# Mixture of experts on one core: the transposes of the activations queued behind the preceding down product, and the 64-slot blocks from the third block on

## The chip, the cores and the metric

The kernel is one program on one core of a Trainium2 chip. The core has a matrix engine (TensorE, PE in the rows; PEld are its weight loads), a vector engine (VectorE, DVE), a scalar engine (ScalarE, ACT), GpSimd (POOL), and SyncE (SP), which here issues nearly all weight transfers. Each engine works through its own instructions in order; between engines they wait for one another by semaphores. The metric is the device time of one launch in microseconds (us), lower is better.

## What is computed

The reference is a chain of three transformer blocks over 256 tokens of width 1024. The change touches the last stage alone, a mixture of 8 experts with 2 experts per token:

```
logits = h @ router
top_v, top_i = lax.top_k(logits, 2)
gates = sum(one_hot(top_i) * softmax(top_v))
for e in range(8):
    out = out + gates[..., e:e+1] * ((silu(h @ we_gate[e]) * (h @ we_up[e])) @ we_down[e])
```

Each expert has three weight matrices of 1024 x 3584 (we_gate, we_up) and 3584 x 1024 (we_down) in float32.

## The kernel before

**Precision.** A large product is done in three matmuls of a fast float type: a weight tile `raw` is split into a rounded high part `whi` (ScalarE, line 306) and the remainder `wlo` (VectorE, line 307), and the activations likewise into two parts. `split_w` does this for a transferred tile of 1 MB in two pieces of 128x1024. The pool of `whi` and `wlo` has 4 buffers each, so a fifth split waits until the matmuls that read the first are done.

**Experts.** The routing decides which tokens go to which expert; each expert takes 128 slots (kind F) or 64 slots (kind N), sorted so that the experts with more tokens get the F places. Of 8 experts 4 are F and 4 are N. Each expert is cut into 7 blocks of 512 hidden columns, so there are 28 F blocks and 28 N blocks. An F block uses the three-matmul form with split weights. An N block uses the float32 weights as they are transferred, in one slower matmul each, and has no splits.

**One block** (function `experts`, one turn of the loop) is: the gate product into `g` (`up_proj`, 2 transfers of 1 MB), the up product into `up` (2 transfers), then the down product **of the block before** into `y` (`down_proj`, 2 transfers), then silu of `g` (ScalarE, line 290, tile `act`) and its product with `up` (VectorE, line 1615, `act`). The activations must be turned for the down product: `act_split` transposes `act` on TensorE into `aT` (line 1642; 4 transposes for F, 2 for N), and copies the result to `an` (N, ScalarE line 1645) or splits it into `ah` (ScalarE line 1649) and `al` (VectorE line 1650) (F). In the kernel before, `act_split` of a block is called in the next turn, between that block's gate and up product, and `ah` is tied behind the first split of that time (`splits_done[LEAD]`).

**Order of blocks.** `seq` starts with HEAD F blocks, then alternates N and F, and ends with the N blocks that are left. Before the first N block the kernel must have sorted the experts (`order`, a chain of some 30 small VectorE instructions on tile `so`), gathered the tokens of the second expert (`one_hots`, tile `sel`; `gather`, 32 matmuls into `xe`), and read the sorted expert numbers into registers of SyncE (`values_load`, line 1623), since all but the first expert's weights are addressed by them. The transfers that follow this read in SyncE's order can't be issued before it.

**What sets the order.** A scheduler orders each engine's instructions from the program's order, priorities and readiness; `issue_after` adds an edge that keeps the instructions of a `with` block behind a given one on its own engine. It costs no instruction. Transferred tiles live in a ring of 12 buffers of 1 MB (15 until the turn `i == HEAD`).

A second pass of the same code for experts with too many tokens is behind a branch and is not run.

Of the kernel before, what the change touches and what calls it, by code (L numbers as in the profile page):

```python
# [11 lines left out]
F32 = mybir.dt.float32  # L12
# [3 lines left out]
AF = mybir.ActivationFunctionType  # L16
OP = mybir.AluOpType
# [9 lines left out]
KINDS = "FNFNFNFN"  # L27
GROUPS = ((0,), (1,), (2, 3), (4, 5), (6, 7))
TAGS = ("u", "u", "x2", "u", "x2")
HEAD = 3  # L30
PE_TAPS = 13
EARLY = 7
PRE = 2
# [3 lines left out]
MORE = 2  # L37
EARLY_RAW = 5
FIRST = 3
LEAD = 0  # L40
HT0 = 1
PB = {"A": 3, "S": 2, "T": 1, "P": 2}
UB = {"u": 22, "u2": 10, "h": 8, "x2": 8}
# [166 lines left out]
class Build:  # L210
# [86 lines left out]
    def split_w(self, raw, n):  # L297

        nc = self.nc
        out = []  # L300
        self.splits_done = []
        for o in range(0, n, 1024):
            w = min(1024, n - o)
            hi = self.wpool.tile([128, 1024], R32, name="whi", tag="whi")
            lo = self.wpool.tile([128, 1024], R32, name="wlo", tag="wlo")
            self.splits_done.append(nc.scalar.activation(hi[:, :w], raw[:, o:o + w], AF.Copy))  # L306
            nc.vector.tensor_tensor(lo[:, :w], raw[:, o:o + w], hi[:, :w].bitcast(F32), op=OP.subtract)  # L307
            out.append((hi, lo))
        return out

# [1239 lines left out]
    def down_proj(self, e, b, act, yp):  # L1550
        nc = self.nc
        for part in range(2):
            raw = self.load_w(self.weights("we_down", e, 2 * b + part))
            if KINDS[e] == "N":
                for k in range(2):
                    st = act[:, k * 128 + part * 64:k * 128 + part * 64 + 64]
                    for n in range(2):
                        nc.tensor.matmul(yp[0][64 * n:64 * n + 64, :], st,  # L1558
                                         raw[:, k * 1024 + n * 512:k * 1024 + (n + 1) * 512],
                                         start=b == 0 and part == 0 and k == 0, stop=b == 6 and part == 1 and k == 1)  # L1560
                continue
            ah, al = act
            w = self.split_w(raw, 2048)
            for k in range(2):
                kk = part * 2 + k
                sh, sl = ah[:, kk * 128:(kk + 1) * 128], al[:, kk * 128:(kk + 1) * 128]
                for n in range(2):
                    h, l = (t[:, n * 512:(n + 1) * 512] for t in w[k])
                    for q, (s, m) in enumerate(((sh, h), (sl, h), (sh, l))):
                        nc.tensor.matmul(yp[n], s, m, start=b == 0 and kk == 0 and q == 0,  # L1570
                                         stop=b == 6 and kk == 3 and q == 2)

    def experts(self, rnd, nxt):


        nc = self.nc
        blocks = {k: [(e, b) for e in range(8) if KINDS[e] == k for b in range(7)] for k in "FN"}
        seq = blocks["F"][:HEAD]
        for n, f in zip(blocks["N"], blocks["F"][HEAD:]):
            seq += [n, f]  # L1580
        seq += blocks["N"][28 - HEAD:]
        at = {group[0]: g for g, group in enumerate(GROUPS)}
        early = {seq.index((group[0], 0)) - (2 if g == 1 else AHEAD): g for g, group in enumerate(GROUPS) if g}
        back, state, xes, yps, done = {}, {0: nxt}, {}, {}, None
        last = None
        for i, (e, b) in enumerate(seq):
            kind = KINDS[e]
            if b == 0:
                yps[e] = [self.ps("y0", "S")] + ([self.ps("y1", "P")] if kind == "F" else [])
                if e in at:  # L1590
                    sel, xe = state[at[e]]
                    for m in GROUPS[at[e]]:
                        xes[m] = xe
            pg = self.pa("g")
            self.up_proj("we_gate", e, b, xes[e], pg)
            if b == 0 and i and e in at:
                back.update(self.back(at[e], sel, TAGS[at[e]]))
            if last:
                act = self.act_split(*last[:2])
            pu = self.pa("up")  # L1600
            self.up_proj("we_up", e, b, xes[e], pu)
            if i == 0:
                back.update(self.back(0, sel, TAGS[0]))
            if done:
                self.combine(*done)
                done = None
            if last:
                self.down_proj(last[0], last[2], act, yps[last[0]])
                if last[2] == 6:
                    done = last[0], yps[last[0]], back[last[0]]  # L1610
            gs = back[e][1]
            w = 512 if kind == "F" else 256
            t = self.stile("act")[:, 0:w]
            self.gate_act(t, pg[:, 0:w], AF.Silu, scale=gs[1])
            nc.vector.scalar_tensor_tensor(t, pu[:, 0:w], gs[1], t, op0=OP.mult, op1=OP.mult)  # L1615
            last = (e, t, b)
            if rnd == 0 and i == 0:
                self.order()
            if i in early:
                g = early[i]  # L1620
                state[g] = self.gather(g, self.one_hots(g, rnd, TAGS[g]), TAGS[g])
            if rnd == 0 and i == HEAD - 2:
                self.ids = [None] + [nc.values_load(self.ci[0:1, p:p + 1], engines=[mybir.EngineType.SP],
                                                    min_val=0, max_val=7) for p in range(1, 8)]
            if rnd == 0 and i == HEAD:
                self.over = nc.values_load(self.ci[0:1, 8:9], min_val=0, max_val=256)
                self.first.__exit__(None, None, None)
                self.ring = [p for p in self.ring if p is not self.rpool3]
                self.epool = self.late.enter_context(self.tc.tile_pool(name="e", bufs=1, reuse_waits="tile"))
        act = self.act_split(*last[:2])  # L1630
        if done:
            self.combine(*done)
        self.down_proj(last[0], last[2], act, yps[last[0]])
        self.combine(last[0], yps[last[0]], back[last[0]])

    def act_split(self, e, t):

        nc = self.nc
        pt = self.ps("aT", "T")
        m = 4 if KINDS[e] == "F" else 2  # L1640
        for k in range(m):
            nc.tensor.transpose(pt[:, k * 128:(k + 1) * 128], t[:, k * 128:(k + 1) * 128], self.con("ident"))  # L1642
        if m == 2:
            an = self.stile("an")
            nc.scalar.activation(an[:, 0:256], pt[:, 0:256], AF.Copy)
            return an
        ah, al = self.stile("ah", dt=R32), self.stile("al", dt=R32)
        with self.tc.issue_after(self.splits_done[LEAD].ins):
            nc.scalar.activation(ah, pt, AF.Copy)  # L1649
        nc.vector.tensor_tensor(al, pt, ah.bitcast(F32), op=OP.subtract)  # L1650
        return ah, al

# [44 lines left out]
```

## Time and profile before

| | us |
|---|---|
| median of 3 runs (lowest, highest) | 1925.13 (1917.29, 1928.01) |
| profiled execution, its own time | 1928.41 |
| its span, first to last instruction | 1926.6 |

The mixture of experts takes the span from about 1011 us to the end. The profile gives the busy time and waits of each engine; a wait is named "engine tile line <- engine tile line", who waited and what ended the wait. "x" counts instructions. PEclk is the granted clock of TensorE as a share of full speed.

### The profile page before, as it was taken

The page shows a single profiled execution, that of the slowest core. Times are in us where ns is not written, and L with a number is a line of the kernel's source. Part 1 is how long each engine was busy: PE and PEld are TensorE (multiplying, and loading weights), DVE is VectorE, ACT ScalarE, POOL GpSimd, SP SyncE. Part 2 cuts the span into 40 slices and gives each one's busy share as a digit, 9 for nine tenths or more (in the row PEclk, how much of TensorE's full clock was granted, in tenths as well). Part 3 has the DMA queues.
Part 4 walks back from the last instruction along what each step waited for, and adds up shares of the span by engine and source line. Part 5 has one row for each costly group of instructions (what it writes and reads, how often), then busy time and mean ns, then how long its engine had stood idle before and what let it go on. Part 6 is the DMA issues. An engine that isn't in the chain of part 4 may idle for free. (4 is left out here: it accounts for less than half of the span.)

```text
span 1926.6 us, 30904 instructions
## 1 busy us (share of the span) xinstructions
PE 1849.0 (96%) x12304; PEld 1517.2 (79%) x12304; DVE 1209.3 (63%) x1814; ACT 963.9 (50%) x1429; POOL 10.9 (1%) x30
## 2 busy tenths in 40 slices
PE   7999999999999999999999999999999999999997
PEld 7989998889999889999788666666665657665654
DVE  7689797765568966655669545655464646454532
ACT  5545555554455774445657444444444435353531
POOL 0000000000000000000000000000000000000000
PEclk9999999999999999999999999999999999999999
DMA  8765566345553235557263999999999999999994
GB/s 300 267 245 198 205 255 245 135 153 178 196 177 119 104 121 186 184 174 256 87 241 130 420 420 421 390 402 393 399 378 388 382 384 390 368 412 371 403 394 162
DMA packets 77657, 531.31 MB, mean 276 GB/s; under 512 B 9283, under 2 KB 10051, under 8 KB 15425
## 3 DMA queue, kind: packets, MB, share of 16 engines
q1 hardware_dynamic: 75168, 524.66, 70.6%
q0 software_dynamic: 1328, 3.29, 0.9%
q8 instruction: 98, 1.61, 0.3%
q10 hardware_dynamic: 1008, 1.31, 0.2%
q14 instruction: 55, 0.44, 0.1%
HBM read 526.60 MB, written 2.62 MB: 275 GB/s over the span
## 5 line engine op out<-in xcount | busy, mean ns | idle before, releaser
L307 DVE TENSOR_TENSOR wlo<-raw,whi 128x1024 fp32r<-128x1024 f32 x618 | 725.1, 1205 | 279.7 <-ACT whi L306 277.1
L306 ACT ACTIVATE whi<-raw 128x1024 fp32r<-128x1024 f32 x618 | 626.8, 1044 | 367.2 <-PE lin L326 249.6
L326 PE MATMUL lin<-hh,whi 128*128 128x256 f32 x1248 | 356.2, 286 | 10.3 <-ACT whi L306 8.1
L326 PE MATMUL lin<-hh,wlo 128*128 128x256 f32 x1248 | 353.5, 284 | 1.8 <-DVE wlo L307 1.8
L326 PE MATMUL lin<-hl,whi 128*128 128x256 f32 x1248 | 353.7, 284 | 0.3
L326 PEld LDWEIGHTS lin<-hh,whi 128*128 128x128 f32 x1248 | 236.8, 190 | 15.4 <-ACT whi L306 9.1
L326 PEld LDWEIGHTS lin<-hh,wlo 128*128 128x128 f32 x1248 | 237.0, 190 | 4.0 <-DVE wlo L307 2.5
L326 PEld LDWEIGHTS lin<-hl,whi 128*128 128x128 f32 x1248 | 237.5, 190 | 2.8 <-issue 1.5
L1547 PE MATMUL g<-whi,xe 128*128 128x512 f32 x448 | 139.4, 392 | 0.3 <-DVE so L1392 0.3
L1547 PE MATMUL up<-whi,xe 128*128 128x512 f32 x448 | 139.5, 392 | 0.0
L1615 DVE SCALAR_TENSOR_TENSOR act<-up,gs,act 128x512 f32<-128x512 f32 (+1 forms) x56 | 34.6, 617 | 165.8 <-PE up L1539 128.1
L1570 PE MATMUL y<-whi,ah 128*128 128x512 f32 x224 | 94.3, 421 | 29.8 <-ACT whi L306 29.8
L1558 PE MATMUL y<-raw,an 128*64 128x512 f32 x448 | 106.7, 603 | 0.0
L1539 PE MATMUL up<-raw,xn 128*64 128x256 f32 x896 | 103.1, 380 | 0.0
L1539 PE MATMUL g<-raw,xn 128*64 128x256 f32 x896 | 102.8, 382 | 0.0
L1649 ACT ACTIVATE ah<-aT 128x512 fp32r<-128x512 f32 x28 | 16.7, 595 | 166.3 <-PE aT L1642 166.3
L1547 PEld LDWEIGHTS g<-whi,xe 128*128 128x128 f32 x448 | 83.9, 188 | 18.8 <-ACT whi L306 0.4
L1547 PEld LDWEIGHTS up<-whi,xe 128*128 128x128 f32 x448 | 84.0, 188 | 17.7
L290 ACT ACTIVATE act<-g,gs 128x512 f32<-128x512 f32 (+1 forms) x56 | 32.5, 581 | 122.2 <-PE g L1539 81.9
L1570 PE MATMUL y<-whi,al 128*128 128x512 f32 x224 | 91.4, 408 | 0.0
L1539 PEld LDWEIGHTS up<-raw,xn 128*64 128x64 f32 x896 | 63.5, 137 | 33.0 <-issue 0.9
L1547 PE MATMUL up<-wlo,xe 128*128 128x512 f32 x224 | 89.2, 398 | 0.0
(467 smaller groups left out, 3193.6 us busy)
## 6 DMA issues: line engine op xcount, KB each, us to landing
raw<-we_gate SPq DMA_DIRECT2D x112, 1024.0 KB, 7.9
raw<-we_up SPq DMA_DIRECT2D x112, 1024.0 KB, 8.6
raw<-we_down SPq DMA_DIRECT2D x112, 1024.0 KB, 7.3
raw<-w_in SPq DMA_DIRECT2D x35, 1024.0 KB, 6.2
raw<-w_ff SPq DMA_DIRECT2D x32, 1024.0 KB, 4.9
raw<-ada_w SPq DMA_DIRECT2D x24, 1024.0 KB, 4.9
raw<-cv_w_gate SPq DMA_DIRECT2D x11, 1024.0 KB, 4.8
raw<-cv_w_up SPq DMA_DIRECT2D x11, 1024.0 KB, 4.8
```

The source lines that it names most:

```text
L290: self.last_gate = self.nc.scalar.activation(*args, **kw)
L306: self.splits_done.append(nc.scalar.activation(hi[:, :w], raw[:, o:o + w], AF.Copy))
L307: nc.vector.tensor_tensor(lo[:, :w], raw[:, o:o + w], hi[:, :w].bitcast(F32), op=OP.subtract)
L326: nc.tensor.matmul(o, s, m, start=start and n == 0, stop=stop and n == 2, skip_group_check=True)
L1539: nc.tensor.matmul(ps[64 * h:64 * h + 64, 0:256], xe["N"][:, kk, :], raw[:, k * 512 + h * 256:k * 512 + (h + 1) * 256], start=kk == 0, sto ...
L1547: nc.tensor.matmul(ps, s, m, start=n == 0, stop=n == 23)
L1558: nc.tensor.matmul(yp[0][64 * n:64 * n + 64, :], st, raw[:, k * 1024 + n * 512:k * 1024 + (n + 1) * 512], start=b == 0 and part == 0 and k ...
L1570: nc.tensor.matmul(yp[n], s, m, start=b == 0 and kk == 0 and q == 0, stop=b == 6 and kk == 3 and q == 2)
L1615: nc.vector.scalar_tensor_tensor(t, pu[:, 0:w], gs[1], t, op0=OP.mult, op1=OP.mult)
L1649: nc.scalar.activation(ah, pt, AF.Copy)
```

## The change

The call of `act_split` moves from the next turn to the end of the block's own turn, right behind the product that makes `act`. So that the transposes are not put ahead of the down product that is emitted just before, they and the N copy `an` get edges behind that product's last matmul and, where it was an F block's, behind the last `whi` of its splits (`self.queued`). The N blocks' `act` on VectorE gets an edge behind the last `wlo` of these splits (`self.low_done`). The tie of `ah` to a split goes. HEAD becomes 2, so that the sequence is F F, then 26 times N F, then N N (before: F F F, 25 times N F, N N N).

```
-HEAD = 3
+HEAD = 2
...
-LEAD = 0
...
-            nc.vector.tensor_tensor(lo[:, :w], raw[:, o:o + w], hi[:, :w].bitcast(F32), op=OP.subtract)
+            self.low_done = nc.vector.tensor_tensor(lo[:, :w], raw[:, o:o + w], hi[:, :w].bitcast(F32), op=OP.subtract)
...
-                        nc.tensor.matmul(yp[n], s, m, start=b == 0 and kk == 0 and q == 0,
-                                         stop=b == 6 and kk == 3 and q == 2)
+                        self.downs = nc.tensor.matmul(yp[n], s, m, start=b == 0 and kk == 0 and q == 0,
+                                                      stop=b == 6 and kk == 3 and q == 2)
...
-        last = None
+        last, self.queued = None, []
...
-            if last:
-                act = self.act_split(*last[:2])
             pu = self.pa("up")
...
                 self.down_proj(last[0], last[2], act, yps[last[0]])
+                self.queued = [self.downs] + ([self.splits_done[-1]] if KINDS[last[0]] == "F" else [])
...
             self.gate_act(t, pg[:, 0:w], AF.Silu, scale=gs[1])
-            nc.vector.scalar_tensor_tensor(t, pu[:, 0:w], gs[1], t, op0=OP.mult, op1=OP.mult)
+            with self.after(*([self.low_done] if kind == "N" and last and KINDS[last[0]] == "F" else [])):
+                nc.vector.scalar_tensor_tensor(t, pu[:, 0:w], gs[1], t, op0=OP.mult, op1=OP.mult)
+            act = self.act_split(e, t)
             last = (e, t, b)
...
-        act = self.act_split(*last[:2])
...
-        for k in range(m):
-            nc.tensor.transpose(pt[:, k * 128:(k + 1) * 128], t[:, k * 128:(k + 1) * 128], self.con("ident"))
-        if m == 2:
-            an = self.stile("an")
-            nc.scalar.activation(an[:, 0:256], pt[:, 0:256], AF.Copy)
-            return an
+        with self.after(*self.queued):
+            for k in range(m):
+                nc.tensor.transpose(pt[:, k * 128:(k + 1) * 128], t[:, k * 128:(k + 1) * 128], self.con("ident"))
+            if m == 2:
+                an = self.stile("an")
+                nc.scalar.activation(an[:, 0:256], pt[:, 0:256], AF.Copy)
+                return an
         ah, al = self.stile("ah", dt=R32), self.stile("al", dt=R32)
-        with self.tc.issue_after(self.splits_done[LEAD].ins):
-            nc.scalar.activation(ah, pt, AF.Copy)
+        nc.scalar.activation(ah, pt, AF.Copy)
```

The lines after are one less than before (306 becomes 305, and so on). What the change does to the engines' order is seen at three places.

**TensorE, one plain N block and the down product behind it.** `y<-raw,an` is the down product of an N block, `y<-whi,ah` of an F block; `g<-raw,xn` and `up<-raw,xn` are the N block's. Before:

```order
L1558 MATMUL y_18211<-raw,an 64x512 x4
L1642 MATMUL aT<-consts,act 128x128
L1558 MATMUL y_18211<-raw,an 64x512 x4
L1642 MATMUL aT<-consts,act 128x128 x3
L1539 MATMUL g<-raw,xn 64x256 x16
L1539 MATMUL up<-raw,xn 64x256 x16
L1642 MATMUL aT<-consts,act 128x128 x2
L1570 MATMUL y_17760<-whi,ah 128x512
```

After (the F block's 24 down matmuls are cut to the first and the last two):

```order
L1557 MATMUL y_16409<-raw,an 64x512 x8
L1642 MATMUL aT<-consts,act 128x128 x4
L1538 MATMUL g<-raw,xn 64x256 x16
L1538 MATMUL up<-raw,xn 64x256 x16
L1569 MATMUL y_16034<-whi,ah 128x512
...
L1569 MATMUL y_16034<-wlo,ah 128x512
L1569 MATMUL y_16035<-wlo,ah 128x512
L1642 MATMUL aT<-consts,act 128x128 x2
L1546 MATMUL g<-whi,xe 128x512 x2
```

The N block's two transposes moved from ahead of the F block's down product to behind it, and the F block's four stand together.

**ScalarE, the same pair of blocks.** `act<-g,gs 128x256` is the N block's silu, `128x512` the F block's. Before:

```order
L1649 ACTIVATE ah<-aT 128x512
L290 ACTIVATE act<-g,gs 128x256
L1645 ACTIVATE an<-aT 128x256
L306 ACTIVATE whi<-raw 128x1024 x10
L290 ACTIVATE act<-g,gs 128x512
L306 ACTIVATE whi<-raw 128x1024 x2
```

After:

```order
L1648 ACTIVATE ah<-aT 128x512
L289 ACTIVATE act<-g,gs 128x256
L305 ACTIVATE whi<-raw 128x1024 x6
L1645 ACTIVATE an<-aT 128x256
L305 ACTIVATE whi<-raw 128x1024 x4
L289 ACTIVATE act<-g,gs 128x512
L305 ACTIVATE whi<-raw 128x1024 x2
```

The four splits of the F block's down weights, and two of the next gate weights, moved ahead of `an`.

**VectorE and SyncE, the start of the experts.** After the first F block's `act`, VectorE before and then after (`so` is the sorting chain, `sel` the token selection that the gather reads, `al` is of the first block):

```order
L1615 SCALAR_TENSOR_TENSOR act<-up,gs,act 128x512
L1407 TENSOR_REDUCE so<-so 128x8
L307 TENSOR_TENSOR wlo<-raw,whi 128x1024
L1406 TENSOR_TENSOR so<-so,rt 128x64
L307 TENSOR_TENSOR wlo<-raw,whi 128x1024
```

```order
L1614 SCALAR_TENSOR_TENSOR act<-up,gs,act 128x512
L1406 TENSOR_REDUCE so<-so 128x8
L1405 TENSOR_TENSOR so<-so,rt 128x64
L1457 TENSOR_SCALAR sel<-consts,so 128x128
L1406 TENSOR_REDUCE so<-so 128x8
L1457 TENSOR_SCALAR sel<-consts,so 128x128
L1405 TENSOR_TENSOR so<-so,rt 128x64
L1406 TENSOR_REDUCE so<-so 128x8
L1405 TENSOR_TENSOR so<-so,rt 128x64
L1457 TENSOR_SCALAR sel<-consts,so 128x128
L1406 TENSOR_REDUCE so<-so 128x8
L1457 TENSOR_SCALAR sel<-consts,so 128x128
```

SyncE's transfers ahead of the first read of an expert number, before and then after (without the first eight before and the first four after, which are gate and up tiles of the first blocks):

```order
L282 DMA raw<-we_gate 128x2048
L282 DMA raw<-we_down 128x2048
L282 DMA raw<-we_gate 128x2048
L282 DMA raw<-we_down 128x2048
L282 DMA raw<-we_up 128x2048 x2
L282 DMA raw<-we_down 128x2048 x2
L1623 TENSOR_LOAD so
```

```order
L281 DMA raw<-we_gate 128x2048 x2
L281 DMA raw<-we_up 128x2048 x2
L281 DMA raw<-we_down 128x2048 x3
L281 DMA raw<-we_gate 128x2048 x2
L281 DMA raw<-we_up 128x2048 x2
L1623 TENSOR_LOAD so
```

The sorting chain now runs without splits in between, and the gather of the second expert stands on TensorE right behind the first F block's `up` and transposes, ahead of the second F block's `g`, where before the second block's three products came first. Ahead of the read there are 15 expert transfers instead of 16.

## Rows read from the trace of the kernel before

**Rows 1.** The page: the span, the matrix engine, and one of the three kinds of expert transfers (count, KB each, median us from issue to landing).

```profile
span 1926.6 us, 30904 instructions
PE 1849.0 (96%) x12304; PEld 1517.2 (79%) x12304; DVE 1209.3 (63%) x1814; ACT 963.9 (50%) x1429; POOL 10.9 (1%) x30
...
raw<-we_gate SPq DMA_DIRECT2D x112, 1024.0 KB, 7.9
```

**Rows 2.** Busy time by stretch (start:end and length in us, then PE, PEld, DVE, ACT, POOL busy with counts, PEclk, DMA share, GB/s).

```profile
1060.00:1200.00 140.00, 135.18 (x761) 91.99 (x761) 70.45 (x78) 62.06 (x80) 0.00 (x0) 0.99 1.01 420
1200.00:1900.00 700.00, 660.17 (x3614) 446.68 (x3614) 367.15 (x396) 306.76 (x375) 1.05 (x2) 0.99 0.98 387
```

**Rows 3.** Waits from 1060 to 1900 us (who waited <- what ended it: us in total, times, longest).

```profile
PE y L1570 <- ACT whi L306: 29.8, 21, 1.4
...
PE aT L1642 <- DVE act L1615: 11.8, 18, 0.7
PEld y L1570 <- DVE wlo L307: 10.9, 22, 0.7
...
ACT whi L306 <- DMA raw<-we_down: 2.2, 4, 0.6
```

**Rows 4.** TensorE in order of time over one plain pair of blocks (start, us from the first start to the last end, operation, count, idle time just before and what ended it).

```profile
1321.46 3.62 PE L1539 MATMUL up<-raw,xn 128*64 128x256 f32 x32
1325.74 0.44 PE L1642 MATMUL aT<-consts,act 128*128 128x128 f32 x2 [0.66 <-DVE act L1615]
1327.59 0.50 PE L1570 MATMUL y<-whi,ah 128*128 128x512 f32 x1 [1.42 <-ACT whi L306]
...
1333.55 0.62 PE L1547 MATMUL g<-whi,xe 128*128 128x512 f32 x2
...
1344.62 1.94 PE L1558 MATMUL y<-raw,an 128*64 128x512 f32 x8
...
1348.62 0.55 PE L1642 MATMUL aT<-consts,act 128*128 128x128 f32 x3
1349.09 3.67 PE L1539 MATMUL g<-raw,xn 128*64 128x256 f32 x32
1352.60 1.68 PE L1539 MATMUL up<-raw,xn 128*64 128x256 f32 x14
```

**Rows 5.** ScalarE at the same place.

```profile
1321.68 0.47 ACT L290 ACTIVATE act<-g,gs 128x256 f32<-128x256 f32 x1 [3.02 <-PE g L1539]
...
1326.49 7.85 ACT L306 ACTIVATE whi<-raw 128x1024 fp32r<-128x1024 f32 x8
```

**Rows 6.** VectorE at the same place.

```profile
1325.20 0.48 DVE L1615 SCALAR_TENSOR_TENSOR act<-up,gs,act 128x256 f32<-128x256 f32 x1 [5.82 <-PE up L1539]
1327.57 11.44 DVE L307 TENSOR_TENSOR wlo<-raw,whi 128x1024 fp32r<-128x1024 f32 x10 [1.89 <-ACT whi L306]
```

**Rows 7.** TensorE where the same work ran without a wait: an F block's down product from its first matmul to the gather behind it; that gather to the next gate product; an N block's down product and the four transposes behind it in one piece.

```profile
1036.31 0.39 PE L1570 MATMUL y<-whi,ah 128*128 128x512 f32 x1
...
1041.81 0.63 PE L1481 MATMUL xe<-sel,hth 128*128 128x256 f32 x4
...
1045.82 0.50 PE L1547 MATMUL g<-whi,xe 128*128 128x512 f32 x1
...
1218.73 3.65 PE L1558 MATMUL y<-raw,an 128*64 128x512 f32 x16
1222.32 0.66 PE L1642 MATMUL aT<-consts,act 128*128 128x128 f32 x4
1222.91 1.30 PE L1539 MATMUL g<-raw,xn 128*64 128x256 f32 x10
```

**Rows 8.** Busy time in short stretches, each around one F block's down product (columns as in Rows 2): the first, the second and the last of six such from 1060 us on, and the first matmul of that product and of the next gate product in the second of them.

```profile
1130.00:1140.00 10.00, 8.58 (x31) 6.43 (x32) 8.19 (x8) 8.30 (x9) 0.00 (x0) 0.83 1.01 419
1488.00:1497.00 9.00, 7.67 (x25) 5.84 (x26) 7.63 (x7) 7.58 (x9) 0.00 (x0) 0.81 1.01 422
...
1877.00:1887.00 10.00, 8.52 (x33) 6.14 (x34) 4.93 (x5) 4.86 (x6) 0.00 (x0) 0.83 1.01 417
...
1489.28 0.51 PE L1570 MATMUL y<-whi,ah 128*128 128x512 f32 x1 [1.42 <-ACT whi L306]
...
1496.82 0.62 PE L1547 MATMUL g<-whi,xe 128*128 128x512 f32 x2
```

**Rows 9.** The start of the experts: the second F block's gate product on TensorE, VectorE's `act` of the first block and parts of its sorting chain, SyncE's transfers ahead of and behind the read of the expert numbers, and TensorE's last down product with the combination behind it.

```profile
1024.65 0.70 PE L1547 MATMUL g<-whi,xe 128*128 128x512 f32 x2 [0.35 <-DVE so L1392]
...
1026.63 0.74 DVE L1615 SCALAR_TENSOR_TENSOR act<-up,gs,act 128x512 f32<-128x512 f32 x1
...
1038.65 0.17 DVE L1422 CAST so<-so 128x8 int32<-128x8 f32 x1
...
1039.38 0.21 DVE L1407 TENSOR_REDUCE so<-so 128x8 f32<-128x64 f32 x1
...
1040.55 2.36 DVE L307 TENSOR_TENSOR wlo<-raw,whi 128x1024 fp32r<-128x1024 f32 x2
...
992.93 3.17 SPq L282 DMA_DIRECT2D raw<-we_down  x2
1043.29 0.95 SPq L282 DMA_DIRECT2D raw<-we_gate  x2
...
1907.39 7.09 PE L1558 MATMUL y<-raw,an 128*64 128x512 f32 x32
```

More of the change, by code (lines that the diff above doesn't have):

```diff
@@ L1557, in down_proj @@
                     for n in range(2):
-                        nc.tensor.matmul(yp[0][64 * n:64 * n + 64, :], st,
-                                         raw[:, k * 1024 + n * 512:k * 1024 + (n + 1) * 512],
-                                         start=b == 0 and part == 0 and k == 0, stop=b == 6 and part == 1 and k == 1)
+                        self.downs = nc.tensor.matmul(yp[0][64 * n:64 * n + 64, :], st,
+                                                      raw[:, k * 1024 + n * 512:k * 1024 + (n + 1) * 512],
+                                                      start=b == 0 and part == 0 and k == 0, stop=b == 6 and part == 1 and k == 1)
                 continue
```

## The prediction, written before the changed kernel ran

> **What bounds the kernel now.** The page comes first: TensorE is busy for 96% of the span, so what the kernel can gain are TensorE's idle spells and its slow stretches. Busy time by stretch shows where they are: from 1060 to 1900 us TensorE is busy 135.2 + 660.2 = 795.3 of 840 us, so about 45 us are idle there [rows 2]. The same rows show transfers at a share of 0.98 and more, which looks like a second bound. The waits say otherwise: in these 840 us the longest of the waits for an expert's transfer adds up to 2.2 us, while the F blocks' down product waited 29.8 us for the high part of its weights, in 21 places, and the N blocks' transposes 11.8 us for `act`, in 18 [rows 3]. So the matrix engine's order binds, and the transfers run a little ahead of it.
>
> The order of time in one plain pair of blocks shows how the two waits hang together [rows 4 to 6]. The N block's up product ends at about 1325.1 (32 matmuls from 1321.46, as its gate product takes 1352.60 - 1349.09 = 3.51). TensorE then stands 0.66 us until VectorE has made `act`, transposes, and stands 1.42 us more until the first `whi` of the down weights. That split starts only at 1326.49, though ScalarE had nothing to do since 1322.15: it is queued behind `an`, and `an` waits for the transposes. Two things come after it. The down product takes 1333.55 - 1327.59 = 5.96 us, where without a wait it took 1041.81 - 1036.31 = 5.50 [rows 4, 7], because VectorE's remainders come too late as well (PEld waits for `wlo` at 22 places [rows 3]). And in some pairs the clock falls right behind the idle spell: in six short stretches of 8 to 10 us the granted clock averages about 0.8, so part of the matmuls there ran at 1.2 GHz instead of 2.4, and the down product took 1496.82 - 1489.28 = 7.54 us [rows 8].
>
> **The change, part by part.** *The N block's transposes and `an`.* They now stand behind the F block's down product. ScalarE can split the down weights when the N block's silu is done. I walk through it with times from the end of the N gate product, at 0. Silu is done at 0.7 [rows 5]. Four `whi` at 0.98 each (7.85 for 8) end at 1.7, 2.7, 3.6 and 4.6; `wlo` at 1.14 each (11.44 for 10 [rows 6]) end at 2.8, 4.0, 5.1 and 6.3. TensorE ends the up product at 3.6 and the down product wants a new split every 5.50 / 4 = 1.37 us: at 3.6, 5.0, 6.3 and 7.7. All four are there, so both idle spells go and the product runs in 5.5, to 9.1. `act`, now held behind the last `wlo`, is done at 6.8, before the transposes at 9.1 want it. Gains, over the places that the waits count: 29.8 + 11.8 us idle, and 21 x (5.96 - 5.50) = 9.7 us of slow product. The six falls of the clock stand behind these idle spells; without them they go too: 6 x (7.54 - 5.96), about 9 us.
>
> *What is behind the moved instructions.* ScalarE's third split of the next gate weights now waits behind `an`, which can start at 9.5. It ends at 10.9 and its remainder at 12.0; TensorE, in the gate product since 9.5, wants the high part at 12.2 and the low part at 12.7. It fits with some 0.6 us to spare, so I take a small loss, 2 us in all; it is 0 at least, and 0.5 us a pair, 13 us, if each hand-over costs a little more than walked.
>
> *The F block's transposes in one piece.* Before, one stands in the middle of the N block's down product and three behind: 1349.09 - 1344.62 = 4.47 us for both [rows 4]. In one piece they took 1222.91 - 1218.73 = 4.18 [rows 7]. The gain is 0.3 us in each of about 21 pairs, 6.3.
>
> *HEAD.* The blocks are the same, in another order; 26 pairs instead of 25. What costs is the start. Before, the second F block's products (TensorE from 1024.65) cover the sorting chain, which VectorE draws out between splits until 1040.5 [rows 9]. After, the gather stands ahead of them, so TensorE waits. `act` of the first block ends at 1027.3. Eight instructions of the chain took 1.17 us where no split stood between (1039.38 to 1040.55), 0.15 each; about 17 of them and `al` (0.7) stand ahead of the first `xn` evacuation, so it comes at 1030.5 and the fourth, ten instructions on, at 1032. The second gate product then starts at about 1033 rather than 1024.65. Of these 8.4 us the gather itself (1045.82 - 1041.81 = 4.0 [rows 7]) and a transpose of 0.4 are only moved: 4 us are lost. The bounds are 2.8 (the gather starts as soon as `act` is there) and 7 (two falls of the clock of 1.5 us each behind the idle spell); I add one such fall, 5.5 in all.
>
> *SyncE.* The chain's result for its registers is ready at about 1030 instead of 1038.8, so the transfers behind the read start some 8.5 us sooner than 1043.29, at about 1034.6 [rows 9]. The first N block wants its first tile at about 1050.5 (1033 and three products of 5.5 to 5.7), and one tile takes 7.9 us to land [rows 1], so nothing waits for it.
>
> *Can the transfers follow?* 3 x 112 tiles less the 15 issued ahead leave 321 of 1.0486 MB [rows 1]. At the 420 GB/s that lasted for 140 us [rows 2] they take 2.5 us each, 801 us, and are in at 1838. The last tile is wanted half a down product before the last combination, which on the changed path comes near 1845. So they just follow, with little to spare. The Trainium skill speaks against this change here: "DMA: Bandwidth & Descriptors", section Where 436 GB/s comes from, lets HBM-to-SBUF transfers be bound by about 358 GB/s a core. By that page's figure the 321 tiles would take 940 us, an estimate, and nothing could be gained. The rows disagree: 420 for 140 us and 387 for 700.
>
> **Sum.** -29.8 - 11.8 - 9.7 - 9 - 6.3 = -66.6; +5.5 at the start, +2 behind `an`: -59. From the profiled execution's own 1928.4 that gives 1869; it lies 3.3 above the median of the runs shown (1925.1), so I forecast 1866 us.
>
> **Rivals.** *The transfers become the bound.* For: a plain pair moves 12 tiles, which take 30.0 us at 420 GB/s, and on the changed path lasts 31.1 - 2.9 = 28.2, so the lead shrinks in plain pairs and only gathers and combinations give it back. If the rate stays halfway, at 404, the tiles take 833 us from 1034.6 and the end is 1868 plus some 16 for the last half product and the combination and output behind it: 1884 span, 1883 as a median. *Nothing gained, because 387 GB/s was all the transfers could do:* 321 tiles take 870 us, the end is at about 1920, no change. Against it: 420 was held while TensorE asked for it, and waits for transfers are nearly absent. *Slower, a new wait:* the splits of the next gate weights find the ring of four full, and the one behind `an` comes late. Each us beyond the 0.6 to spare costs 26 us over the pairs. From 0.6 + 59/26 = 2.9 us late the change loses; at 3.5 us late it would be about 1940. For it speaks only that `an` now stands in the middle of the splits. *The edges do little,* since the scheduler had other reasons for its order: the order of the changed kernel shows that they do move the rows.
>
> **How the numbers follow.** My forecast, 1855 to 1890, has 0.68; the transfers at a lower rate, 1883 to 1910, 0.16; no change 0.08; slower 0.06; the rest lies below 1855. A change under 0.5% (9.6 us) can't be told from none with this kernel. Faster by more than that, below 1915.5, holds 0.86, the same 0.07, slower 0.07. The range reaches from 1850, the transfers' own end (1838 + 14, less the offset to the median), to 1905, inside the rival with the slower transfers.
>
> **What would show it.** In the profile after: the waits of `y` for `whi` and of `aT` for `act` fall from 41.6 us to under 5; a plain pair takes 28 to 28.5 us from up product to up product instead of 31.14; the granted clock shows no fall in the plain pairs; TensorE has 3 to 9 us of idle time between 1024 and 1033; the rate from 1200 us on rises from 387 to above 405 GB/s. I am wrong if TensorE's waits for transferred tiles (`g<-raw`, `up<-raw`, ScalarE's `whi` for a DMA) grow to tens of us, or if the next gate product waits for `whi` or `wlo` in each pair.

## The result, and the profile after

| | before | after |
|---|---|---|
| median, us (lowest, highest) | 1925.58 (1917.29, 1928.01) | 1862.51 (1858.88, 1863.49) |
| ratio to before, with its 95% interval | | 0.9679 (0.9651 to 0.9707) |
| profiled execution, its own time, us | 1928.41 | 1858.88 |
| its span, us | 1926.6 | 1857.0 |

The change saves 63 us, 3.2%. The page of the profile after, with the lines that answer to [rows 1]:

```profile
span 1857.0 us, 30774 instructions
PE 1817.5 (98%) x12304; PEld 1505.6 (81%) x12304; DVE 1207.7 (65%) x1814; ACT 960.9 (52%) x1429; POOL 10.8 (1%) x30
...
raw<-we_gate SPq DMA_DIRECT2D x112, 1024.0 KB, 11.0
```

Busy time by stretch, as in [rows 2], to 1840 us, where the tail now begins:

```profile
1060.00:1200.00 140.00, 139.63 (x791) 95.55 (x790) 75.06 (x79) 66.21 (x83) 0.00 (x0) 1.00 1.01 417
1200.00:1840.00 640.00, 635.52 (x3599) 440.59 (x3597) 362.23 (x393) 301.67 (x373) 1.05 (x2) 1.00 1.00 414
```

TensorE is idle for 4.9 of 780 us, before for 45 of 840. The waits from 1060 to 1840 us, which answer to [rows 3]:

```profile
PEld y L1557 <- DMA raw<-we_gate: 8.1, 25, 0.4
PEld y L1569 <- ACT whi L305: 6.9, 18, 0.4
PEld y L1569 <- DVE wlo L306: 6.2, 6, 1.7
...
PE y L1569 <- DVE wlo L306: 3.8, 3, 1.3
...
PEld g L1546 <- DVE wlo L306: 2.2, 6, 0.4
```

No matmul waits for `whi` any more and no transpose for `act`. What is left lies in the weight loads, which overlap matmuls, in three waits for `wlo`, and in 1.0 us in which the gathers wait for their tokens (`xn`). One plain pair on TensorE, then ScalarE and VectorE at the same place, as in [rows 4 to 6]:

```profile
1293.85 0.71 PE L1546 MATMUL g<-whi,xe 128*128 128x512 f32 x2
...
1308.60 0.66 PE L1642 MATMUL aT<-consts,act 128*128 128x128 f32 x4
1309.18 3.67 PE L1538 MATMUL g<-raw,xn 128*64 128x256 f32 x32
1312.69 3.62 PE L1538 MATMUL up<-raw,xn 128*64 128x256 f32 x32
1316.24 0.50 PE L1569 MATMUL y<-whi,ah 128*128 128x512 f32 x1
1316.58 0.40 PE L1569 MATMUL y<-whi,al 128*128 128x512 f32 x1
...
1321.86 0.38 PE L1642 MATMUL aT<-consts,act 128*128 128x128 f32 x2
1322.00 0.71 PE L1546 MATMUL g<-whi,xe 128*128 128x512 f32 x2
```

```profile
1312.91 0.48 ACT L289 ACTIVATE act<-g,gs 128x256 f32<-128x256 f32 x1 [3.02 <-PE g L1538]
1313.28 3.89 ACT L305 ACTIVATE whi<-raw 128x1024 fp32r<-128x1024 f32 x4
...
1322.28 0.39 ACT L1645 ACTIVATE an<-aT 128x256 f32<-128x256 f32 x1 [2.36 <-PE aT L1642]
```

```profile
1314.36 4.63 DVE L306 TENSOR_TENSOR wlo<-raw,whi 128x1024 fp32r<-128x1024 f32 x4 [3.75 <-ACT whi L305]
1318.91 0.48 DVE L1614 SCALAR_TENSOR_TENSOR act<-up,gs,act 128x256 f32<-128x256 f32 x1
...
1323.64 1.23 DVE L306 TENSOR_TENSOR wlo<-raw,whi 128x1024 fp32r<-128x1024 f32 x1 [1.99 <-ACT whi L305]
```

The pair, gate product to gate product, takes 1322.00 - 1293.85 = 28.15 us; before, a pair took 31.14, up product to up product [rows 4]. The down product starts with the end of the up product, and the transposes follow it without a wait. The first four `whi` are done at 1317.17, and `an` runs at 1322.28, when nothing waits behind it but the next split.

**A measure for parts of the kernel.** Up to the first `cnt` matmul of the sorting chain all kernels here run the same instructions on TensorE, VectorE and ScalarE, but for `two_matmuls`, where the first block's shortened products stand ahead of it. Yet the `cnt` matmul starts at 1014 us in one execution and at 1024 in another (the last section has a part of it). So the tables below also give the *experts' part*: the span less the start of that matmul. Before it is 1926.6 - 1023.71 = 902.9 us, after it is 1857.0 - 1014.14 = 842.9: 60.0 us less.

### The profile page after: what moved, and what is told of

Read it like the earlier page. It is cut to its first block, busy times and chain, and to the rows that moved or that the text cites. A ratio compares the mean times of both kernels' runs of the same rounds, so it can differ in the third digit from the quotient of the medians.

```text
span 1857.0 us, 30774 instructions
## 1 busy us (share of the span) xinstructions
PE 1817.5 (98%) x12304; PEld 1505.6 (81%) x12304; DVE 1207.7 (65%) x1814; ACT 960.9 (52%) x1429; POOL 10.8 (1%) x30
## 5 line engine op out<-in xcount | busy, mean ns | idle before, releaser
L325 PEld LDWEIGHTS lin<-hh,whi 128*128 128x128 f32 x1248 | 237.6, 190 | 14.9 <-ACT whi L305 8.8
L1557 PE MATMUL y<-raw,an 128*64 128x512 f32 x448 | 102.3, 599 | 0.5 <-ACT an L1645 0.5
L1569 PE MATMUL y<-whi,ah 128*128 128x512 f32 x224 | 90.3, 403 | 0.0
L1546 PE MATMUL g<-wlo,xe 128*128 128x512 f32 x224 | 89.2, 398 | 0.0
L1538 PEld LDWEIGHTS g<-raw,xn 128*64 128x64 f32 x896 | 61.8, 137 | 33.0 <-issue 3.8
```

The source lines that it names most:

```text
L325: nc.tensor.matmul(o, s, m, start=start and n == 0, stop=stop and n == 2, skip_group_check=True)
L1538: nc.tensor.matmul(ps[64 * h:64 * h + 64, 0:256], xe["N"][:, kk, :], raw[:, k * 512 + h * 256:k * 512 + (h + 1) * 256], start=kk == 0, sto ...
L1546: nc.tensor.matmul(ps, s, m, start=n == 0, stop=n == 23)
L1557: self.downs = nc.tensor.matmul(yp[0][64 * n:64 * n + 64, :], st, raw[:, k * 1024 + n * 512:k * 1024 + (n + 1) * 512], start=b == 0 and pa ...
L1569: self.downs = nc.tensor.matmul(yp[n], s, m, start=b == 0 and kk == 0 and q == 0, stop=b == 6 and kk == 3 and q == 2)
```

## Experiments

Each ratio is to the kernel before as it ran beside that kernel on the same chip, so it need not be the quotient of two medians of this table.

| kernel | median, us | ratio to before (95%) | span | first `cnt` at | experts' part |
|---|---|---|---|---|---|
| before | 1925.58 | | 1926.6 | 1023.71 | 902.9 |
| after | 1862.51 | 0.9679 (0.9651 to 0.9707) | 1857.0 | 1014.14 | 842.9 |
| head2_only | 1931.24 | 1.0034 (1.0012 to 1.0057) | 1926.8 | 1017.23 | 909.6 |
| no_low_edge | 1880.86 | 0.9778 (0.9738 to 0.9818) | 1879.2 | 1021.55 | 857.6 |
| splits_first | 1879.78 | 0.9771 (0.9728 to 0.9815) | 1879.1 | 1023.79 | 855.3 |
| no_queue_edges | 1870.66 | 0.9722 (0.9691 to 0.9753) | 1865.6 | 1016.01 | 849.6 |
| half_n_transfers | 1862.92 | 0.9678 (0.9640 to 0.9717) | 1867.9 | 1023.73 | 844.2 |
| two_matmuls | 1852.77 | 0.9634 (0.9593 to 0.9675) | 1851.4 | 1014.68 | 836.7 |
| edges_head3 | 1864.34 | 0.9702 (0.9662 to 0.9742) | 1858.4 | 1018.26 | 840.1 |
| late_combine3 | 1858.20 | 0.9663 (0.9629 to 0.9696) | 1857.4 | 1016.87 | 840.5 |
| after_again | 1865.31 | 0.9690 (0.9665 to 0.9715) | 1866.6 | 1022.31 | 844.3 |
| edges_head3_again | 1864.76 | 0.9682 (0.9657 to 0.9707) | 1862.9 | 1022.12 | 840.8 |
| late_combine | 1861.70 | 0.9676 (0.9651 to 0.9701) | 1859.9 | 1018.48 | 841.4 |
| late_combine3_again | 1864.60 | 0.9686 (0.9663 to 0.9709) | 1858.2 | 1018.08 | 840.1 |

### HEAD alone

```
-HEAD = 3
+HEAD = 2
```

(in the kernel before)

> The kernel before with HEAD = 2 and nothing else of the change. My theory: the gather ahead of the second gate product costs 4 to 6 us of TensorE idle time at the start (from the first count matmul to the second gate product 9 us longer, of which 4.4 us are moved work), and the waits of y for whi and of aT for act stay at about 40 us or more: 1930 us (1927 to 1934). Rival, the gain came from HEAD, because the transfers behind the read of the expert numbers start some 8 us sooner: below 1910.

Measured: 1931.24 us, slower by 0.34%. Two waits from 1060 to 1840 us show that the stalls stay (the kernel before has the same 26.9 and 10.5 us in this window, which is 60 us shorter than that of [rows 3]):

```profile
PE y L1570 <- ACT whi L306: 26.9, 19, 1.4
PE aT L1642 <- DVE act L1615: 10.5, 16, 0.7
```

HEAD = 2 costs 6.7 us in the experts' part and gains nothing by itself. So the edges and the moved call gain 909.6 - 842.9 = 66.7 us, or 909.6 - 844.3 = 65.3 against the changed kernel's second profile (`after_again`). The second is the fairer number: the granted clock over the 12 us from the first `cnt` matmul on is 0.72 in both of its kernels, in the changed kernel's first profile 0.86.

### Each half of the reorder without the other

First, VectorE's edge goes. In the plain pairs the order changes in one thing, `act` of the N block stands ahead of the remainders:

```
-            with self.after(*([self.low_done] if kind == "N" and last and KINDS[last[0]] == "F" else [])):
+            if True:
```

> The changed kernel without the edge that holds the N blocks' act on VectorE behind the last remainder of the down weights. VectorE then has act ahead of all twelve remainders, and act waits for the end of the up product. My theory: the first wlo is ready about 1.75 us behind the end of the up product and wanted at 0.9, so some 0.85 us are lost in each of about 26 pairs, with waits of y for wlo of about 20 us: 1885 us (1876 to 1895). Rival, only ScalarE's order and the place of the transposes matter: at most 1867.

Second, the splits go ahead of `an`, but the N transposes stay ahead of the down product (and `act` is free, as above):

```
-        with self.after(*self.queued):
+        late = self.queued if m == 4 else self.queued[1:]
+        with self.after(*(late if m == 4 else [])):
             for k in range(m):
                 nc.tensor.transpose(...)
-            if m == 2:
...
+        if m == 2:
...
+            with self.after(*late):
                 nc.scalar.activation(an[:, 0:256], pt[:, 0:256], AF.Copy)
```

> Only ScalarE's part of the change for the N blocks: an is held behind the four splits of the F block's down weights, but the N transposes stand ahead of the down product as before, and act is not held back. The F blocks' transposes stay in one piece, HEAD = 2. My theory (both parts of the reorder count, each by its own wait): y no longer waits for whi, TensorE waits some 0.66 us for act in each of 26 pairs, 17 us, and the product runs in 5.6: 1880 us (1874 to 1890). Rival A, the place of the transposes is what counts: 1900 or more. Rival B, the transposes' place costs nothing, since the transfers bind: at most 1867.

TensorE in plain pairs of the first kernel, up product to up product:

```profile
1294.03 3.62 PE L1538 MATMUL up<-raw,xn 128*64 128x256 f32 x32
1299.45 0.74 PE L1569 MATMUL y<-wlo,ah 128*128 128x512 f32 x2 [0.65 <-DVE wlo L306]
...
1323.13 3.62 PE L1538 MATMUL up<-raw,xn 128*64 128x256 f32 x32
```

and of the second:

```profile
1297.88 3.62 PE L1538 MATMUL up<-raw,xn 128*64 128x256 f32 x32
1302.16 0.44 PE L1643 MATMUL aT<-consts,act 128*128 128x128 f32 x2 [0.66 <-DVE act L1614]
...
1326.74 3.62 PE L1538 MATMUL up<-raw,xn 128*64 128x256 f32 x32
```

Measured: 1880.86 and 1879.78 us, both where expected. The first pair takes 29.10 us, 0.95 more than in the changed kernel, and the product waits for the low part in it (14.9 us in 20 places from 1060 to 1840 us). The second takes 28.86, 0.71 more, the wait for `act` (11.2 us in 17 places). By the experts' part and by the medians the changed kernel loses 15 to 18 us without VectorE's edge, and 11 to 17 without that edge and with the transposes ahead of the product, where 11 is 855.3 less 844.3, the changed kernel's second profile with the same clock at the start. The two numbers are not to be added: they are one gain, which needs both. With the transposes behind the product but without VectorE's edge the experts' part is 857.6, no shorter than the 855.3 with neither. VectorE's edge with the transposes left ahead was not run. From `head2_only` to `splits_first` the experts' part falls by 909.6 - 855.3 = 54.3 us. Less the 5 us of the F transposes below, about 49 us are what ScalarE gains by splitting before `an`, the clock's falls included. The tie of `ah` to a split, which is gone as well, has no part in it: in a plain pair of either kernel ScalarE waits for `aT` ahead of `ah` (7.44 us in `head2_only`, 7.12 in `splits_first`). The rivals that give all to one half fall.

### The F blocks' transposes in one piece

```
-        with self.after(*self.queued):
+        if True:
```

> The changed kernel without the edges behind the down product and its splits (the call of act_split stays where the change put it, and act on VectorE stays behind the last remainder). In this kernel the scheduler puts only the F blocks' transposes elsewhere: one in the middle of the N block's down product, three behind it, as before. It prices that one term. My theory: 0.3 us in each of 26 pairs, 1870 us (1867 to 1873). Rival, the split costs nothing: 1862 to 1864.

```profile
1289.15 3.62 PE L1538 MATMUL up<-raw,xn 128*64 128x256 f32 x32
...
1309.65 1.94 PE L1557 MATMUL y<-raw,an 128*64 128x512 f32 x8
1311.51 0.33 PE L1642 MATMUL aT<-consts,act 128*128 128x128 f32 x1
1311.77 1.94 PE L1557 MATMUL y<-raw,an 128*64 128x512 f32 x8
1313.64 0.55 PE L1642 MATMUL aT<-consts,act 128*128 128x128 f32 x3
...
1317.62 3.62 PE L1538 MATMUL up<-raw,xn 128*64 128x256 f32 x32
```

ScalarE in the same pair:

```profile
1289.74 3.89 ACT L305 ACTIVATE whi<-raw 128x1024 fp32r<-128x1024 f32 x4
...
1298.74 0.39 ACT L1645 ACTIVATE an<-aT 128x256 f32<-128x256 f32 x1 [2.36 <-PE aT L1642]
```

Measured: 1870.66 us. The pair takes 28.47, 0.32 more. Beside the changed kernel's second profile, whose start has the same low clock, the experts' part is 5.3 us longer. The edges behind the down product are worth this and no more: with VectorE's edge alone the scheduler puts the N transposes behind the product, and `an` behind the four splits, by itself. So with the call moved, that one edge gives all of the change but these 5 us.

### TensorE's order or the transfers

Three kernels ask which of the two binds now. Half of the N blocks' transfers left out (the same line in `down_proj`):

```
-            raw = self.load_w(self.weights(name, e, 2 * b + part))
+            if KINDS[e] == "F" or part == 0:
+                raw = self.load_w(self.weights(name, e, 2 * b + part))
```

> The changed kernel with half the transfers of the N blocks left out: their gate, up and down products use the first transferred tile of a block twice, so 84 of some 321 tiles behind the read of the expert numbers are not moved, and the output is another. TensorE's work is the same. My theory, the transfers just follow and TensorE's order bounds: only the waits for raw go (9 us of weight loads), 1858 us (1853 to 1864). Rival, the transfers are the bound of the changed kernel: 84 tiles of 2.5 us are 210 us less, so the time falls by tens of us, below 1840.

A third of the F blocks' gate and up matmuls left out:

```
-                for s, m in ((xh, h), (xl, h), (xh, l)):
-                    nc.tensor.matmul(ps, s, m, start=n == 0, stop=n == 23)
+                for s, m in ((xh, h), (xh, l)):
+                    nc.tensor.matmul(ps, s, m, start=n == 0, stop=n == 15)
```

> The changed kernel without the matmul of the activations' low part in the F blocks' gate and up products (16 matmuls instead of 24; the output is less exact). It takes 448 matmuls of 0.23 us, 103 us, off TensorE and leaves every transfer, so it shows where the transfers' own end lies. My theory: 321 tiles of 1.0486 MB at 418 to 421 GB/s take 800 to 805 us, from 1025.8 in the changed kernel's profile to 1829, with 14 to 16 us of products and output behind the last: 1843 us (1836 to 1852), with waits for raw of tens of us. Rival A, the transfers have room to spare at a higher rate: 1765 to 1790. Rival B, they already set the end: 1858 or more.

The edges with the old HEAD, where the transfers behind the read start later:

```
-HEAD = 2
+HEAD = 3
```

> The changed kernel with HEAD = 3 as before: the edges alone. My theory, TensorE's order bounds: the 4.6 us that the start lost in the changed kernel come back, 1858 us (1855 to 1861). Rival, the transfers have become the bound: they start about 8 us later again and the end moves with them, 1866 to 1871, with waits of g, up and y for raw of more than 8 us.

With half the transfers: 1862.92 us and an experts' part of 844.2, no change. So TensorE's order binds, as said.

With 103 us of TensorE's work less: 1852.77 us, just above my interval, and only 10 us gained. Its busy time by stretch:

```profile
1060.00:1830.00 770.00, 737.27 (x3954) 452.55 (x3953) 436.30 (x470) 366.97 (x455) 1.05 (x2) 1.00 1.01 420
```

The longest waits for transfers of SyncE, which issues them, from 1060 to 1840 us:

```profile
SPq L281 <- DMA raw<-we_down: 110.7, 70, 2.1
SPq L281 <- DMA raw<-we_up: 105.6, 63, 2.6
SPq L281 <- DMA raw<-we_gate: 105.2, 60, 2.0
```

The busy share of its DMA engines from 1800 to 1850 us, in tenths, in 40 slices of 1.25 us:

```profile
DMA  9999999999999999999999976665100000199110
```

The rate stays at 420 GB/s, so no higher one showed when TensorE asked for it. SyncE, which in the changed kernel waits for buffers and only 2.2 us for transfers, now waits 322 us for transfers under way. They run from 1028.98 to about 1835, and the last down product starts at 1835.51: some 806 us, as expected (800 to 805). Three small sizes make the miss: a start 3 us later, 3 us more of transfers, and 16 us behind the last tile instead of 14. But this kernel doesn't show the transfers alone. In its plain pairs the splits hold TensorE back (`g` and `up` wait 25 us for `wlo`), and one takes 1339.64 - 1311.61 = 28.03 us, as in the changed kernel. A good part of the 103 us went there; how much can't be told apart.

With HEAD = 3 I expected the 4.6 us of the start back, 1858 us. 1864.34 us, and 1864.76 in a second run, say no; the experts' part is 2.8 to 3.5 us shorter (2 to 4 was expected of the second run). Its DMA engines, in the same slices:

```profile
DMA  9999999999999999999999999999966655200000
```

and TensorE's last two down products:

```profile
1839.55 1.94 PE L1557 MATMUL y<-raw,an 128*64 128x512 f32 x8 [0.46 <-DMA raw<-we_down]
...
1842.39 1.94 PE L1557 MATMUL y<-raw,an 128*64 128x512 f32 x8 [0.53 <-ACT an L1645]
1844.51 1.94 PE L1557 MATMUL y<-raw,an 128*64 128x512 f32 x8 [0.19 <-DMA raw<-we_down]
```

The transfers run from 1038.62 to about 1843, again 804 us, and the last products wait for their tiles. The rival was right in kind (the end moves with the transfers) and too large in size: it had 1866 us or more, and over 8 us of waits for tiles. So the two limits lie within a few us of each other: HEAD = 2 pays 4 to 6 us at the start and buys transfers that start 9 us sooner.

### Two attempts at a faster kernel

In the three pairs with the combination of an N expert, VectorE's additions to `x` stand ahead of the remainders of the down weights, and the changed kernel's down product waits (VectorE, then TensorE):

```profile
1258.22 1.41 DVE L1668 TENSOR_TENSOR x<-x,cmb 128x256 f32<-128x256 f32 x4 [1.60 <-PE cmb L1664]
1259.55 4.62 DVE L306 TENSOR_TENSOR wlo<-raw,whi 128x1024 fp32r<-128x1024 f32 x4
```

```profile
1260.82 0.74 PE L1569 MATMUL y<-wlo,ah 128*128 128x512 f32 x2 [1.26 <-DVE wlo L306]
```

`late_combine3` and `late_combine` (HEAD 3 and 2) call `combine` behind the next down product:

```
-            if done:
-                self.combine(*done)
-                done = None
+            ready, done = done, None
             if last:
                 self.down_proj(last[0], last[2], act, yps[last[0]])
...
+            if ready:
+                self.combine(*ready, self.downs)
...
-                        nc.tensor.matmul(ps, t[:, c * 128:(c + 1) * 128], ...)
+                        with self.after(*late):
+                            nc.tensor.matmul(ps, t[:, c * 128:(c + 1) * 128], ...)
```

> The changed kernel with HEAD = 3, and with the matmuls of an N expert's combination held behind the next down product, so that VectorE makes the remainders of the F block's down weights ahead of its additions to x. It is meant to take away the 1.3 us that y waits for wlo in each of three pairs of the changed kernel. My theory, TensorE's order bounds: about 3 to 4 us below edges_head3, 1860.5 us (1857 to 1864), no waits of y for wlo over 0.5 us. Rival, with HEAD = 3 the transfers bind: no change against edges_head3, and longer waits for raw. Rival, the additions now delay the remainders of the next gate weights by as much: no change, with waits of g for wlo.

> The changed kernel (HEAD = 2), with the matmuls of an N expert's combination held behind the next down product. Theory: with the transfers' earlier start TensorE's order still bounds, so the three waits for wlo of 1.3 us go and the experts' part falls from 843 to 839 to 840 us; the median is 3 to 4 us below the changed kernel's. Rival: VectorE's additions now delay the remainders of the next gate weights by as much: 843 us, with waits of g for wlo.

Three more runs, beside `late_combine` on one chip, repeat kernels from above:

> The changed kernel once more, beside the three below on the same chip. Expected: 1862.5 us (1859 to 1866), and 843 us from the first count matmul of the sorting chain to the end of the span, as in its first profile. Ahead of the experts the instructions of all these kernels are the same, and still the 256-column matmuls between some 700 and 830 us of the profiles took 113.3 ns each in some and 117.8 ns in others. If the pace belongs to the program, this profile has 113.3 there again, as the first one of this kernel; if it belongs to the execution, it may have 117.8, and then its span is up to 6 us longer with the experts' part unchanged.

> The changed kernel with HEAD = 3 once more. Theory: the transfers that start some 12 us later take back part of what the start gains, so the experts' part is 840 us (839 to 842), 2 to 4 less than with HEAD = 2, and the medians of the two are within 4 us of each other. Rival, nothing is taken back: 838 us and a median 4 to 6 us below the changed kernel's.

> HEAD = 3 and the combinations held back, once more. By the trace of its first run the experts' part was as long as that of edges_head3 (840.5 and 840.1 us), though its median was 6 us lower. Theory: transfers bind in both, so the experts' part is 840 to 841 us again and the median within 3 us of edges_head3 on the same chip. Rival, the lower median was real: 4 to 6 us below it.

The waits of `y` for `wlo` go (0.8 us of `g` for `wlo` come in their place), and with HEAD = 2 the experts' part falls by 2.9 us against the profile with the same low clock at the start, 844.3 to 841.4 (839 to 840 was expected). With HEAD = 3 it stays at 840.1 to 840.5, as it was without this edit: there the transfers set the end. So the first median of `late_combine3` lay where it was expected, but not for the reason given; the rival was right. On one chip the four medians are 1865.31, 1864.76, 1861.70 and 1864.60 us with overlapping intervals, so none is measurably better than the changed kernel, and the 1858.2 us of the first run of `late_combine3` did not come back.

## Why the prediction was right, point by point

The forecast was 1866 us, the result 1862.5.

- **What bounds.** Right. Without half of the N transfers the time is the same, and the stalls named are gone: 41.6 us of waits of `y` for `whi` and `aT` for `act` became none on TensorE.
- **The walk through a pair.** From the end of the N gate product, 1312.69, the rows give for the fourth `whi` 4.5 (said 4.6), the fourth `wlo` 6.3 (6.3), `act` 6.7 (6.8), the transposes 9.2 (9.1), the start of `an` 9.6 (9.5) and the remainder of the third gate split 12.2 (12.0). 28.15 us a pair lies in the 28 to 28.5 forecast.
- **Product in 5.50.** It took 1321.86 - 1316.24 = 5.62. Its first matmul takes 0.34 us to the next, the others 0.23; its weight load is not ahead of it (`PEld y<-whi`, 0.4 at most). What holds the load is open: `whi` had long been done. This term was too large by 0.12 x 21 = 2.5 us.
- **Clock.** No fall in the plain pairs: PEclk 1.00 in both stretches.
- **Behind `an`.** Priced at 2 us, cost none on TensorE: the gate product waits only in its weight loads, 2.2 us. What the walk did not have are the three waits behind the combinations, 3.8 us.
- **F's transposes.** 0.3 us a pair said, 0.32 measured.
- **Sum of the edges.** -66.6 + 2 = -64.6 us said; -65.3 to -66.7 between `head2_only` and the changed kernel. That it comes so near is in part luck, since the terms miss both ways: the product and F's transposes gave 2.5 and 1 us less than said, and the waits behind the combinations were in no term, while `head2_only` lost more to the clock than the six falls counted (PEclk 0.98 from 1060 to 1840 us, in the changed kernel 1.00).
- **The start.** 5.5 us said. TensorE around it:

```profile
1014.14 0.37 PE L1386 MATMUL cnt<-rt,consts 128*128 128x8 f32 x2
...
1017.86 1.11 PE L1642 MATMUL aT<-consts,act 128*128 128x128 f32 x4 [3.13 <-DVE act L1614]
1018.76 0.58 PE L1480 MATMUL xe<-sel,hth 128*128 128x256 f32 x1
...
1024.05 0.62 PE L1546 MATMUL g<-whi,xe 128*128 128x512 f32 x2
```

  The second gate product starts 9.9 us behind the count matmul, 9.3 said; before it was 0.94, and 4.4 of it is moved work, so 4.6 us are lost. The idle time, 3.3 us, lies in the forecast 3 to 9. But the working had a step wrong: the gather did not wait for VectorE's last evacuations. It began right behind the transposes, and took 5.3 us because part of it ran at the low clock (PEclk 0.79 from 1016 to 1024). In `after_again` the clock is lower there (0.66 from 1024 to 1034) and the start costs about 1.5 us more. So the forecast had 4 us of waits and one fall of 1.5; there was one wait for `act` of 3.1 us and a fall of about 1.3. The size was right, the second wait was not there. `head2_only`, with the lower clock at its start, puts HEAD alone at 6.7.
- **SyncE.** The first transfer behind the read comes 1025.80 - 1014.14 = 11.7 us behind the count matmul, before 43.29 - 23.71 = 19.6 [rows 9]: 7.9 us sooner, 8.5 said.
- **Transfers just follow, with little to spare.** Right, and closer than it looked: 414 to 417 GB/s, landing in 11.0 instead of 7.9 us, and an end of their own that takes over as soon as they start 9 us later. The prediction's 1838 for the last tile is 1836 by its own terms (1034.6 + 801), which changes nothing. The rate of about 358 GB/s of the Trainium skill's "DMA: Bandwidth & Descriptors", section Where 436 GB/s comes from, did not bind here; the rows show 420.
- **Rivals.** That 387 GB/s was all falls with 414. A new wait behind `an` did not come. That the edges do little falls with `head2_only`: the blocks' order alone costs 0.3%. Of the edges behind the down product and its splits it nearly holds: with the call moved, VectorE's edge alone gives all but 5 us (`no_queue_edges`).
- **The remaining 3.5 us** of the result are in no term. The experts' part fell by 60.0 us, or 58.6 in the second profile, against 59 forecast. In the profiles the rest lies ahead of the experts, in code that the change doesn't touch; for the runs without a profile that isn't shown. A second set of runs of the changed kernel has a median of 1865.31 us, so 3.5 us lie within what the same program shows.

## What to carry to other kernels

When an engine has nothing to do and its next instruction is ready, look at what stands ahead of it in its own queue: here one small copy that waited for a late transpose kept four ready weight splits back, and about 49 of 1925 us went there. Moving such a copy pulls at the whole chain: with the splits first on ScalarE, TensorE still waited for VectorE, until VectorE made the remainders first and the transposes stood behind the product. These two are worth 11 to 18 us together, and the second without the first nothing. So find the edge that decides the order; here the one on VectorE made the scheduler set the other engines right, but for 5 us. And when a wait goes, work out when the next resource ends by itself; here the transfers lay a few us behind, and each further mend gained less than its own wait.

## What the runs showed of the hardware

**Two paces of the same matmuls at the same granted clock.** TensorE from 740 to 780 us, in `after` and in `after_again`, which are the same program, in identical work ahead of the experts:

```profile
740.00:780.00 40.00, 40.00 (x355) 40.00 (x355) 28.30 (x31) 20.03 (x23) 0.00 (x0) 1.00 0.52 189
740.00:780.00 40.00, 40.00 (x342) 40.00 (x342) 26.36 (x29) 18.93 (x21) 0.00 (x0) 1.00 0.52 185
```

355 or 342 matmuls in 40 us, 113 or 117 ns each, both at a PEclk of 1.00. The same program had both, so the program alone doesn't set it. Nor does the chip alone: of the four kernels on one chip one had the faster pace (`head2_only`), of the four on another two (`no_queue_edges`, `late_combine3`), on the third none. The cause is open. Over 120 us it makes 4 to 5 us, more than the difference between the last four kernels.

**The clock falls and the idle time ahead of them.** With idle spells of 0.66 and 1.42 us around the transposes some pairs ran with the clock lowered, here one of `head2_only`, as in [rows 8]:

```profile
1140.00:1150.00 10.00, 8.43 (x29) 6.30 (x30) 7.98 (x8) 8.00 (x9) 0.00 (x0) 0.83 1.02 424
```

With 0.66 us alone, in `splits_first`, the clock is 1.00 from 1060 to 1840 us.
